# The second layer's MLP as seven products of quarters, with weight sums on GpSimd

## The chip, the cores and the metric

The kernel runs on one core of a Trainium2 chip. The metric is the device time of one launch in microseconds (us). Engines in the profile are PE (TensorE, matmuls), PEld (its weight loads), DVE (VectorE), ACT (ScalarE), POOL (GpSimd) and SP (SyncE, which issues most DMAs).

## What is computed

One inference step of a trunk of two layers over 640 tokens (512 sample tokens, then 128 prompt tokens), width D = 1024, MLP width 4096, all in float32. The first layer mixes by chunked gating and gated linear attention, the second by a recurrent block; each is followed by a squared-ReLU MLP, and every sub-layer has a norm ahead of it and one behind it:

```python
x = x + g1 * rmsnorm(y, norm_g[i, 1])
hff = rmsnorm(x, norm_g[i, 2]) * (1.0 + sc2) + sh2
f = jnp.square(jax.nn.relu(hff @ mlp_w1[i] + mlp_b1[i])) @ mlp_w2[i] + mlp_b2[i]
x = x + g2 * rmsnorm(f, norm_g[i, 3])
```

The shifts, scales and gates (sh, sc, g) differ between sample and prompt tokens. For the second layer (i = 1) the last line's x is the output.

## The kernel before

Every float32 operand of a large product is the sum of two float32r parts: `split` (L193) casts on ACT (L195) and subtracts on DVE (L196). A product is then three matmuls, `mm3` (L199): first weight part by both parts of the data, second weight part by the first part of the data (L201 to L203).

Weights come in slabs of 128 x 1024, 512 KB each. `prep` loads them in the order of use on SP's queue into raw buffers (three of them, `raw`), splits them and puts both parts into a slot of its class; `done` gives a slot back and calls `prep` again. So loads and splits run ahead as far as slots and raw buffers are free. A scheduler fixes one order of instructions for each engine when the program is built; each engine, and each DMA queue, then works in that order, and an instruction that waits holds what stands behind it.

`chain` (L336) finishes a token tile of 128 tokens: the norm behind a sub-layer (squares summed on ACT L342, products with the gate's rows on DVE L343), the residual x (L354), the next norm (ACT L357), eight transposes on PE (L333), scale and shift into hf (DVE L366, ACT L368), and the split of hf into `h1` and `h2`, feature-major. At the end of the kernel it writes the output instead (L351, L352). The token tiles come to the second MLP in the order 0, 1, 2, 4, 3.

The MLP, `mlp` (L1069), is called once for each layer. First product: a slab of W1 gives 128 of the 4096 hidden features for all tokens, in two halves of 320 tokens (`proj`), each eight feature tiles x 3 matmuls of 320 columns; ten slabs (six at the start, four at the end) go by token groups of 256 and 384 instead (`proj_groups`, `proj_group`), so that the first group can begin before all token tiles are there. ACT makes the square of the ReLU (L1068, L1069), then f is split. Second product: four slabs of W2 give all of y for one group of four hidden tiles; `ytile` makes, per token tile and half of 512 features, 4 x 3 matmuls of 512 columns, token-major, and DVE adds the bank to y in SBUF (L1103). `hgroup` and `ygroup` alternate, eight groups in all. In the last group the first three token tiles are finished (chain, output) ahead of the work on the others (L1129 to L1138).

`run` (L1166 on) ends with `out.send((wp, (1, 3), ExitStack()))`, which projects out of the recurrent block and runs the chains, and `self.mlp(1, mlp_i[1], xs, wp, None)` (L1221), which is the second layer's MLP. PSUM has six product banks and two others in this part. POOL issues the loads of slabs that the first layer had split ahead to memory (L165), the last of them at 862 us, and does nothing after that.

## Time and profile before

| | us |
|---|---|
| median of 3 runs | 1422.86 |
| lowest, highest | 1421.66, 1423.7 |
| span of the profiled execution | 1418.3 |

The span is from the first to the last instruction of one profiled execution. The runs' times lie 3.4 to 5.4 us above it. The mean granted TensorE clock of that execution was 0.998. The second MLP takes the time from about 960 us to the end.

| engine | busy us | share |
|---|---|---|
| PE | 1395.2 | 98% |
| DVE | 881.1 | 62% |
| ACT | 672.7 | 47% |
| POOL | 15.3 | 1% |

In the profile a group's row gives the busy time and the mean duration of one instruction, and then how long the engine was idle just before such instructions and what released it. In a timeline row the first number is the start and the second the duration; several instructions of one form are drawn together as x2, x4 and so on. Matmuls overlap: the time that one takes from the stream is the distance from its start to the next one's.

### The profile page before, as it was taken

The page shows a single profiled execution, that of the slowest core. Times are in us where ns is not written, and L with a number is a line of the kernel's source. Part 1 is how long each engine was busy: PE and PEld are TensorE (multiplying, and loading weights), DVE is VectorE, ACT ScalarE, POOL GpSimd, SP SyncE. Part 2 cuts the span into 40 slices and gives each one's busy share as a digit, 9 for nine tenths or more (in the row PEclk, how much of TensorE's full clock was granted, in tenths as well). Part 3 has the DMA queues.
Part 4 walks back from the last instruction along what each step waited for, and adds up shares of the span by engine and source line. Part 5 has one row for each costly group of instructions (what it writes and reads, how often), then busy time and mean ns, then how long its engine had stood idle before and what let it go on. Part 6 is the DMA issues. An engine that isn't in the chain of part 4 may idle for free.

```text
span 1418.3 us, 20181 instructions
## 1 busy us (share of the span) xinstructions
PE 1395.2 (98%) x8080; PEld 1243.8 (88%) x8080; DVE 881.1 (62%) x1407; ACT 672.7 (47%) x1217; POOL 15.3 (1%) x29
## 2 busy tenths in 40 slices
PE   7999999999999999999999999999999999999998
PEld 4788889889899898898889999879988989989896
DVE  5598858656768777787466798676342442433436
ACT  6744635675244154252267768867341522423142
POOL 2000000000000000000000000000000000000000
PEclk9999999999999999999999999999999999999999
DMA  9545317214577766766302442223231321212102
GB/s 370 177 153 179 130 64 265 92 45 144 168 250 243 264 224 229 272 202 213 138 31 104 153 151 99 89 76 107 102 105 45 104 73 61 99 35 104 60 30 75
DMA packets 60046, 195.89 MB, mean 138 GB/s; under 512 B 5888, under 2 KB 17632, under 8 KB 55344
## 3 DMA queue, kind: packets, MB, share of 16 engines
q1 hardware_dynamic: 57936, 179.92, 36.8%
q0 software_dynamic: 2016, 14.68, 3.0%
q8 instruction: 63, 1.03, 0.3%
q14 instruction: 31, 0.25, 0.1%
HBM read 176.97 MB, written 17.61 MB: 137 GB/s over the span
## 4 chain that ended last, share of the span: by engine, by line
PE 87%; DVE 5%; ACT 5%; issue 2%; DMA 2%; SPq 0%; DVEq 0%; ACTq 0%
PE mm L203 27%; PE mm L202 27%; PE mm L201 27%; PE aux L333 1%; DVE junk L244 1%; PE aux L823 1%; ACT h L195 1%; ACT w L195 1%; PE aux L808 1%; PE aux L442 1%; PE aux L818 1%; ACT r L135 1%; DVE w L196 0%; DMA x<-in_xs 0%; PE aux L681 0%
## 5 line engine op out<-in xcount | busy, mean ns | idle before, releaser
L201 PE MATMUL mm<-h,w 128*128 128x320 f32 (+2 forms) x1376 | 425.8, 310 | 3.4 <-ACT h L195 3.4
L202 PE MATMUL mm<-h,w 128*128 128x320 f32 (+2 forms) x1376 | 426.1, 310 | 0.6 <-DVE h L196 0.6
L203 PE MATMUL mm<-h,w 128*128 128x320 f32 (+2 forms) x1376 | 426.6, 310 | 0.0
L196 DVE TENSOR_TENSOR w<-raw,w 128x1024 fp32r<-128x1024 f32 x164 | 198.8, 1223 | 139.1 <-ACT w L195 138.0
L195 ACT CAST w<-raw 128x1024 fp32r<-128x1024 f32 x164 | 170.4, 1049 | 215.9 <-PE mm L203 120.7
L201 PEld LDWEIGHTS mm<-h,w 128*128 128x128 f32 x1376 | 258.6, 188 | 5.9 <-ACT h L195 3.7
L202 PEld LDWEIGHTS mm<-h,w 128*128 128x128 f32 x1376 | 259.2, 188 | 2.9 <-DVE h L196 1.2
L203 PEld LDWEIGHTS mm<-h,w 128*128 128x128 f32 x1376 | 259.2, 188 | 0.1
L244 DVE SCALAR_TENSOR_TENSOR junk<-raw,cond 128x1024 bf16<-128x1024 f32 x160 | 195.2, 1220 | 37.8 <-DMA raw<-in_modw 36.1
L202 PE MATMUL mm<-w,f 128*128 128x512 f32 x520 | 205.4, 395 | 0.0
L201 PE MATMUL mm<-w,f 128*128 128x512 f32 x520 | 205.1, 395 | 0.0
L203 PE MATMUL mm<-w,f 128*128 128x512 f32 x520 | 204.7, 395 | 0.0
L1103 DVE TENSOR_TENSOR y<-mm,y 128x512 f32<-128x512 f32 x140 | 95.7, 688 | 121.8 <-PE mm L203 121.8
L195 ACT CAST f<-r 128x320 fp32r<-128x320 f32 (+2 forms) x128 | 56.1, 459 | 235.5 <-PE mm L203 233.4
L203 PEld LDWEIGHTS mm<-w,f 128*128 128x128 f32 x520 | 97.6, 188 | 23.4 <-DVE f L196 0.2
L202 PEld LDWEIGHTS mm<-w,f 128*128 128x128 f32 x520 | 97.7, 188 | 22.6 <-DVE w L196 0.3
L201 PEld LDWEIGHTS mm<-w,f 128*128 128x128 f32 x520 | 97.7, 188 | 22.6
L1068 ACT ACTIVATE r<-mm,cols 128x320 f32<-128x320 f32 (+2 forms) x128 | 65.6, 524 | 66.6 <-PE mm L203 65.8
L196 DVE TENSOR_TENSOR f<-r,f 128x320 fp32r<-128x320 f32 (+2 forms) x128 | 60.2, 488 | 49.8 <-ACT f L195 48.7
L201 PE MATMUL mm<-w,h 128*128 128x512 f32 x220 | 86.9, 397 | 0.0
L202 PE MATMUL mm<-w,h 128*128 128x512 f32 x220 | 86.3, 393 | 0.0
L203 PE MATMUL mm<-w,h 128*128 128x512 f32 x220 | 85.6, 393 | 0.6 <-DVE h L196 0.6
(226 smaller groups left out, 1626.7 us busy)
## 6 DMA issues: line engine op xcount, KB each, us to landing
raw<-in_w SPq DMA_DIRECT2D x128, 512.0 KB, 3.4
raw<-in_modw SPq DMA_DIRECT2D x80, 512.0 KB, 4.3
ws<-w SPq DMA_DIRECT2D x14, 1024.0 KB, 5.2
w<-ws POOLq DMA_DIRECT2D x14, 1024.0 KB, 5.1
m<-in_mod SPq DMA_DIRECT2D x8, 1024.0 KB, 12.8
raw<-in_rgin SPq DMA_DIRECT2D x16, 512.0 KB, 4.9
raw<-in_evin_fm SPq DMA_DIRECT2D x12, 512.0 KB, 3.9
x<-in_xs SPq DMA_DIRECT2D x8, 512.0 KB, 5.0
```

The costliest lines, as they stand in the source:

```text
L135: self.tab = nc.scalar.activation(*args, **kw)
L195: i = self.nc.scalar.copy(d1, x)
L196: self.nc.vector.tensor_tensor(d2, x, d1.bitcast(F32), OP.subtract)
L201: nc.tensor.matmul(ps, w1, x1, start=start, stop=False)
L202: nc.tensor.matmul(ps, w1, x2, start=False, stop=False)
L203: nc.tensor.matmul(ps, w2, x1, start=False, stop=stop)
L244: nc.vector.scalar_tensor_tensor(self.junk, r, 1.0, self.cond[:, c, :], op0=OP.mult, op1=OP.mult, accum_out=self.modacc[:, l * 48 + j, c:c ...
L333: self.nc.tensor.transpose(ps[:, i * P:(i + 1) * P], xn[:, k * P:(k + 1) * P], self.ident)
L442: nc.tensor.matmul(ps[32 * j:32 * j + 32, :], cpad[:, kk, :], mods[k][:, kk, :], start=kk < 4, stop=kk >= 4, tile_position=(0, 32 * j))
L808: nc.tensor.matmul(ps[:, d * 256:(d + 1) * 256], ke[d][:, toks(t)], qe[d][:, :, toks(t)], start=True, stop=True)
L1068: nc.scalar.activation(r, ps, AF.Relu, bias=self.col(B1 + l * 32 + m))
L1103: nc.vector.tensor_tensor(ys[t][:, h, :], ps, b2row[:, h, :] if q == 0 else ys[t][:, h, :], OP.add)
```

## The change

The second layer's call of `mlp` is replaced by `smlp`, with its slabs planned by `smlp_plan`. Both matrix products are done by Strassen's scheme in Winograd's form: each of the three matrices is cut in four quarters, and seven products of sums of quarters replace the eight plain ones.

First product: the data's quarters are 4 feature tiles x 320 tokens of `hraw`, which the chains now leave feature-major and unsplit (`chain` writes it in place of hf, and each token tile's x to memory, `xd`). The sums of the data's quarters are four subtractions on DVE of 128 x 1280. The weights' sums are three POOL additions of 128 x 512 for each of 16 pairs of slabs (`sums`), one more for the slab called ya, which reads back a sum that POOL's queue has written to memory. For the first six pairs the products with the plain quarter (0, 0) come first (slabs e, `early`), since they need only the first 320 tokens. Each product is 192 matmuls of 320 columns. What the products add up to is added on DVE out of PSUM (or copied by ACT), and the four quarters of the hidden features stay in SBUF (`z`, 16 tiles of 128 x 2 x 640); ReLU and square on ACT.

Second product: W2's sums are again made on POOL (wb, wc one addition a slab, wa two and a write to memory), z's sums on DVE (t1 to t4) right ahead of their split (`fop`, 16 slots). y is feature-major, so weights stand still and 320 tokens stream. There are three phases of two products each, called b, a, c, in 16 steps of 24 matmuls, and a last product d in 16 steps of 12. At the end of a phase the banks go into y's quarters (`hraw` again): four copies on ACT (e1), 4 + 8 + 8 + 4 + 4 + 4 DVE operations of 128 x 320 (e7, e6, e5, e3, e2, e4). y is then transposed token tile by token tile (`finish`), and `chain` writes the output. Token tiles 3 and 4 are finished during d, tiles 0, 1 and 2 behind its last matmul. PSUM is changed to eight product banks ahead of the second product.

The second MLP has 112 slabs in place of 64, five slots, and a fourth raw buffer (every fourth is `rawx`). In the diff below, removed comments are left out.

```diff
     def raw(self):
+        self.nraw += 1
+        if self.rawx is not None and self.nraw % 4 == 0:
+            return self.rawx.tile([P, D], F32, name="raw", tag="raw", bufs=1)
         return self.rawp.tile([P, D], F32, name="raw", tag="raw", bufs=3)
...
+            if callable(src):
+                src(w)
+            elif i in self.ready:
...
         nc.vector.scalar_tensor_tensor(x, s2, rs, x, op0=OP.mult, op1=OP.add)
+        if self.hraw is not None:
+            nc.sync.dma_start(self.xd[t], x)
...
-        h = wp.tile([P, KD, P], F32, name="hf", tag="hf", bufs=2)
+        if self.hraw is None:
+            h = wp.tile([P, KD, P], F32, name="hf", tag="hf", bufs=2)
+        else:
+            h = self.hraw[:, :, toks(t)]
...
-        self.split(self.h1[:, :, toks(t)], self.h2[:, :, toks(t)], h)
+        if self.hraw is None:
+            self.split(self.h1[:, :, toks(t)], self.h2[:, :, toks(t)], h)
...
+        def sums(p):
+            t, u = self.raw(), self.raw()
+            load(t, lo, W1[2 * p][:, lo])
+            nc.sync.dma_start(u, W1[2 * p + 1])
+            nc.gpsimd.tensor_tensor(u[:, hi], u[:, lo], u[:, hi], OP.add)
+            nc.gpsimd.tensor_tensor(t[:, hi], u[:, hi], t[:, lo], OP.subtract)
+            nc.gpsimd.dma_start(s2d[p], t[:, hi])
+            nc.gpsimd.tensor_tensor(u[:, lo], t[:, lo], u[:, lo], OP.subtract)
+            return t, u
...
+        def wa(s, w):
+            u, t = self.raw(), self.raw()
+            nc.sync.dma_start(u, W2[2 * s])
+            load(t, lo, W2[2 * s + 1][:, hi])
+            nc.gpsimd.tensor_tensor(t[:, lo], u[:, hi], t[:, lo], OP.add)
+            nc.gpsimd.tensor_tensor(t[:, hi], t[:, lo], u[:, lo], OP.subtract)
+            nc.gpsimd.dma_start(s2d[self.NP + s], t[:, hi])
+            both(w, t)
...
+        op((0, 0), B(0, 0))
+        for p in range(NE):
+            ps = self.mm()[:, :HT]
+            prod(ps, ("e", p // 2), p % 2, (0, 0), True, True)
+            nc.scalar.copy(zq(p, 0, 0), ps)
+            if p % 2:
+                done(("e", p // 2))
+        tt(B(0, 1), B(1, 1), B(0, 1), OP.subtract)
+        tt(B(0, 0), B(0, 1), B(0, 0))
+        op((1, 0), B(0, 0))
+        op((0, 1), B(0, 1))
+        tt(B(0, 1), B(0, 0), B(1, 0), OP.subtract)
+        tt(B(0, 0), B(1, 1), B(0, 0), OP.subtract)
+        op((1, 1), B(0, 0))
...
+        for name, first, second in (("b", (0, lambda s: zq(s, 0, 0), e1), (1, t3, e7)),
+                                    ("a", (1, t2, e6), (0, t1, e5)),
+                                    ("c", (1, lambda s: zq(s, 1, 1), e3), (0, lambda s: zq(s, 1, 0), e2))):
+            ba, bb = [], []
+            for s in range(NP + 1):
+                if s < NP:
+                    step(s, (name, s), *first, ba)
+                if s:
+                    step(s - 1, (name, s - 1), *second, bb)
+                    done((name, s - 1))
...
+            if s == 12:
+                finish(3)
+            if s == 14:
+                finish(4)
+        for t in range(3):
+            finish(t)
...
         out.send((wp, (1, 3), ExitStack()))
-        self.mlp(1, mlp_i[1], xs, wp, None)
+        self.retire(self.rw)
         res.close()
-        pes.close()
+        xes.close()
+        self.smlp(1, mlp_i[1])
```

Where the second MLP begins, DVE before (x3 is token tile 3's residual, rs and hf belong to its norm and operand; h2 are second parts of the data's operand, f of the hidden features):

```order
L354 SCALAR_TENSOR_TENSOR x3_2046<-scr_8778,rs_8786,x3_2046 128x1024
L366 TENSOR_SCALAR hf_8682<-aux_8683,modv_122 128x128 x2
L366 TENSOR_SCALAR hf_8682<-aux_8692,modv_122 128x128 x2
L319 RECIPROCAL rs_8793<-sd_8792 128x1
L196 TENSOR_TENSOR h2_126<-hf_8682,h1_125 128x8x128
L366 TENSOR_SCALAR hf_8797<-aux_8798,modv_122 128x128 x2
L366 TENSOR_SCALAR hf_8797<-aux_8807,modv_122 128x128 x2
L196 TENSOR_TENSOR h2_126<-hf_8797,h1_125 128x8x128
L196 TENSOR_TENSOR f_8862<-r_8863,f_8862 128x256
L196 TENSOR_TENSOR f_8893<-r_8894,f_8893 128x256
```

DVE in the same place after, from the operand of tile 4 on (w are slabs, raw_8807 and raw_8818 hold sums of pairs 0 and 1, raw_8954 and raw_8993 of pairs 2 and 3, z0 is the first hidden tile pair):

```order
L381 TENSOR_SCALAR hraw_8480<-aux_8720,modv_154 128x128 x2
L381 TENSOR_SCALAR hraw_8480<-aux_8729,modv_154 128x128 x2
L329 RECIPROCAL rs_8844<-sd_8843 128x1
L205 TENSOR_TENSOR w_8919<-raw_8807,w_8919 128x512
L205 TENSOR_TENSOR w_8919<-raw_8818,w_8919 128x512
L381 TENSOR_SCALAR hraw_8480<-aux_8848,modv_154 128x128 x2
L381 TENSOR_SCALAR hraw_8480<-aux_8857,modv_154 128x128 x2
L1318 TENSOR_TENSOR hraw_8480<-hraw_8480 128x4x320 x2
L205 TENSOR_TENSOR w_8952<-raw_8954,w_8952 128x1024
L205 TENSOR_TENSOR h2_158<-hraw_8480,h1_157 128x4x320
L205 TENSOR_TENSOR w_8991<-raw_8993,w_8991 128x1024
L205 TENSOR_TENSOR h2_158<-hraw_8480,h1_157 128x4x320
```

The per-tile splits of hf are gone; the splits of whole quarters (128x4x320) stand between splits of slabs whose sums POOL makes.

The loads of pairs 2 and 3 on SP's queue after, between the writes of x to memory (none of these rows has a counterpart before):

```order
L366 DMA xd_8483<-x2_2073 128x1024
L1175 DMA raw_8818<-in_w1 128x512
L1185 DMA raw_8819<-in_w1 128x1024
L1175 DMA raw_8953<-in_w1 128x512
L366 DMA xd_8485<-x4_2083 128x1024
L1185 DMA raw_8993<-in_w1 128x1024
L366 DMA xd_8484<-x3_2078 128x1024
L1185 DMA raw_8954<-in_w1 128x1024
L1175 DMA raw_8992<-in_w1 128x512
```

The load into raw_8953 stands ahead of the other loads of these pairs, and a write of x waits between them.

POOL late in phase a after, where the first slab of c comes in between (L1240 to L1242 are a slab of a, L1249 one of c); before, POOL has no row in this part:

```order
L1240 TENSOR_TENSOR raw_11997<-raw_11996,raw_11997 128x512
L1241 TENSOR_TENSOR raw_11997<-raw_11997,raw_11996 128x512
L1242 DMA s2_101<-raw_11997 128x512
L1249 TENSOR_TENSOR raw_12076<-raw_12076 128x512
L1240 TENSOR_TENSOR raw_12037<-raw_12036,raw_12037 128x512
L1241 TENSOR_TENSOR raw_12037<-raw_12037,raw_12036 128x512
```

For each slab of a, two additions and one DMA were added, for each of c one addition.

The end of PE's order before (mm_12223 is the last bank of token tile 4):

```order
L201 MATMUL mm_12223<-xp_6824,f_11879 128x512
L202 MATMUL mm_12223<-wlo_8201,f_11879 128x512
L203 MATMUL mm_12223<-xp_6824,f_11879 128x512
L201 MATMUL mm_12223<-w_11946,f_11910 128x512
L202 MATMUL mm_12223<-w_11946,f_11910 128x512
L203 MATMUL mm_12223<-w_11946,f_11910 128x512
```

and after (mm_12805 is the last bank of product d, L1482 are transposes of y):

```order
L210 MATMUL mm_12805<-h1_157,w_12908 128x320
L211 MATMUL mm_12805<-h2_158,w_12908 128x320
L212 MATMUL mm_12805<-h1_157,w_12908 128x320
L1482 MATMUL mm_13123<-ident_141,hraw_8480 128x128 x4
L1482 MATMUL mm_13128<-ident_141,hraw_8480 128x128
L1482 MATMUL mm_13147<-ident_141,hraw_8480 128x128 x4
L1482 MATMUL mm_13128<-ident_141,hraw_8480 128x128
L1482 MATMUL mm_13152<-ident_141,hraw_8480 128x128 x2
L1482 MATMUL mm_13171<-ident_141,hraw_8480 128x128 x2
L1482 MATMUL mm_13128<-ident_141,hraw_8480 128x128
```

Before, nothing follows the last matmul with weights; after, the transposes of token tiles 0, 1 and 2 do.

## Rows read from the trace of the kernel before

**Rows 1.** The page: PE's busy time, and the chain's shares by line.

```profile
PE 1395.2 (98%) x8080; PEld 1243.8 (88%) x8080; DVE 881.1 (62%) x1407; ACT 672.7 (47%) x1217; POOL 15.3 (1%) x29
PE mm L203 27%; PE mm L202 27%; PE mm L201 27%; PE aux L333 1%; DVE junk L244 1%; PE aux L823 1%; ACT h L195 1%; ACT w L195 1%; PE aux L808 1%; PE aux L442 1%; PE aux L818 1%; ACT r L135 1%; DVE w L196 0%; DMA x<-in_xs 0%; PE aux L681 0%
```

**Rows 2.** Windows; columns: stretch, length, busy PE, PEld, DVE, ACT, POOL, clock, DMA share, GB/s.

```profile
1100.00:1150.00 50.00, 50.00 (x288) 45.83 (x287) 18.73 (x24) 18.35 (x32) 0.00 (x0) 1.00 0.26 85
...
1411.00:1418.30 7.30, 0.36 (x2) 0.00 (x0) 3.12 (x6) 1.02 (x3) 0.00 (x0) 0.84 0.20 76
```

**Rows 3.** Timeline of PE: three starts, 192 and then 120 matmuls apart.

```profile
1047.40 0.31 PE L201 MATMUL mm<-h,xp 128*128 128x320 f32 x1
...
1075.56 0.39 PE L201 MATMUL mm<-w,f 128*128 128x512 f32 x1
...
1103.45 0.31 PE L201 MATMUL mm<-h,xp 128*128 128x320 f32 x1
```

**Rows 4.** Timeline where the second MLP begins: last token tiles' operands.

```profile
961.08 1.50 ACT L368 ACTIVATE hf<-aux,modv 128x128 f32<-128x128 f32 x4
...
972.91 0.16 DVE L319 RECIPROCAL rs<-sd 128x1 f32<-128x1 f32 x1 [1.57 <-ACT sd L135]
...
974.92 1.09 PE L333 MATMUL aux<-ident,scr 128*128 128x128 f32 x8
...
976.44 1.50 ACT L368 ACTIVATE hf<-aux,modv 128x128 f32<-128x128 f32 x4 [0.85 <-DVE hf L366]
...
979.24 0.62 PE L201 MATMUL mm<-h,w 128*128 128x384 f32 x2 [0.75 <-ACT h L195]
980.50 0.44 PE L202 MATMUL mm<-h,w 128*128 128x384 f32 x1 [0.64 <-DVE h L196]
```

**Rows 5.** Groups by line and form, 980 to 1418 us: slab and operand splits.

```profile
L196 DVE TENSOR_TENSOR w<-raw,w 128x1024 fp32r<-128x1024 f32 x41 | 49.8, 1224 | 87.8 <-ACT w L195 87.7
...
L195 ACT CAST w<-raw 128x1024 fp32r<-128x1024 f32 x41 | 42.5, 1047 | 66.8 <-PE mm L203 66.2 <-DMA raw<-in_w 0.5
...
L196 DVE TENSOR_TENSOR f<-r,f 128x320 fp32r<-128x320 f32 x44 | 20.5, 489 | 12.0 <-ACT f L195 11.5
...
L195 ACT CAST f<-r 128x320 fp32r<-128x320 f32 x44 | 19.0, 458 | 149.0 <-PE mm L203 148.5
```

**Rows 6.** DMA issues: count, KB each, median us from issue to landing.

```profile
raw<-in_w SPq DMA_DIRECT2D x128, 512.0 KB, 3.4
```

**Rows 7.** Timeline of POOL, then of DVE, near the kernel's start.

```profile
10.08 1.42 POOL L566 MEMSET attm<- 128x512 f32 x2 [9.63 <-DMA x<-in_xs]
...
18.45 0.63 POOL L575 MEMSET kdt<- 64x640 f32 x1 [0.33 <-PE aux L333]
...
21.27 1.11 POOL L571 MEMSET qe<- 64x640 f32 x1 [1.08 <-PE aux L333]
22.42 0.63 POOL L572 MEMSET qe<- 64x640 f32 x1
...
18.37 1.26 DVE L477 TENSOR_SCALAR x<-x,rs 128x1024 f32<-128x1024 f32 x1
...
21.06 0.75 DVE L477 TENSOR_SCALAR x<-x,rs 128x1024 f32<-128x1024 f32 x1
...
22.10 1.23 DVE L196 TENSOR_TENSOR w<-raw,w 128x1024 fp32r<-128x1024 f32 x1
```

**Rows 8.** Timeline of the kernel's end: last matmul, last token tile on DVE.

```profile
1410.96 0.40 PE L203 MATMUL mm<-w,f 128*128 128x512 f32 x1
...
1412.12 0.69 DVE L343 TENSOR_TENSOR y<-y,grow 128x512 f32<-128x512 f32 x1
...
1413.65 1.42 DVE L351 SCALAR_TENSOR_TENSOR x<-y,rs,x 128x512 f32<-128x512 f32 x2
```

More of the change, by code (lines that the diff above doesn't have):

```diff
@@ L309, in gate_rows @@
         grow = wp.tile([P, 2, D], F32, name="grow", tag="grow", bufs=1)
+        grow = [grow[:, c, :] for c in range(2)]
         self.get_rows((l, part), grow)
@@ L504, in start @@
                 self.put_rows("c", ccol)
-                self.get_rows("c", self.cond)
+                self.get_rows("c", [self.cond[:, c, :] for c in range(2)])
             part_b(k)
@@ L1139, in mlp, with smlp_plan, load, add @@
         es.close()
+    NP = 16
+    NE = 6
+    def smlp_plan(self, l):
+        nc, W1, W2 = self.nc, self.A["w1"][l], self.A["w2"][l]
+        pl, idx = self.plan, {}
+        lo, hi = slice(0, 512), slice(512, D)
+        s2d = [self.dram.tile([P, 512], F32, name="s2") for _ in range(2 * self.NP)]
+        held = {}
+        def load(t, c, src):
+            nc.sync.dma_start(t[:, c], src)
+        def add(key, f):
+            idx[key] = len(pl)
+            pl.append((f, "b"))
+        def sums(p):
[7 more added lines that the diff above has]
+            return t, u
+        def both(w, t):
+            self.split(w[:, 0, :], w[:, 1, :], t)
+        def early(j, w):
+            t = self.raw()
+            for i in range(2):
+                load(t, (lo, hi)[i], W1[2 * (2 * j + i)][:, lo])
+            both(w, t)
+        def late_a(p, w):
+            held[p] = sums(p)
+            both(w, held[p][1])
+        def late_b(j, w):
+            for i, c in enumerate((lo, hi)):
+                self.split(w[:, 0, c], w[:, 1, c], held.pop(2 * j + i)[0][:, hi])
+        def xa(p, w):
+            held[p] = sums(p)
+            both(w, held[p][0])
+        def xb(p, w):
+            both(w, held.pop(p)[1])
+        def ya(p, w):
+            t = self.raw()
+            load(t, lo, W1[2 * p][:, hi])
+            load(t, hi, s2d[p])
+            nc.gpsimd.tensor_tensor(t[:, hi], t[:, lo], t[:, hi], OP.subtract)
+            both(w, t)
+        def yc(j, w):
+            t = self.raw()
+            for i in range(2):
+                load(t, (lo, hi)[i], W1[2 * (2 * j + i) + 1][:, hi])
+            both(w, t)
+        def wb(s, w):
+            t = self.raw()
+            nc.sync.dma_start(t, W2[2 * s])
+            nc.gpsimd.tensor_tensor(t[:, hi], t[:, lo], t[:, hi], OP.subtract)
+            both(w, t)
+        def wa(s, w):
[5 more added lines that the diff above has]
+            nc.gpsimd.dma_start(s2d[self.NP + s], t[:, hi])
+            both(w, t)
+        def wc(s, w):
+            t = self.raw()
+            load(t, lo, W2[2 * s + 1][:, lo])
+            load(t, hi, s2d[self.NP + s])
+            nc.gpsimd.tensor_tensor(t[:, hi], t[:, lo], t[:, hi], OP.subtract)
+            both(w, t)
+        def wd(j, w):
+            t = self.raw()
+            for i in range(2):
+                load(t, (lo, hi)[i], W2[2 * (2 * j + i) + 1][:, hi])
+            both(w, t)
+        def bind(f, i):
+            return lambda w: f(i, w)
+        for j in range(self.NE // 2):
+            add(("e", j), bind(early, j))
+        for j in range(self.NE // 2):
+            for p in (2 * j, 2 * j + 1):
+                add(("xb", p), bind(late_a, p))
+                if p % 2:
+                    add(("s2", j), bind(late_b, j))
+        for p in range(self.NE, self.NP):
+            add(("xa", p), bind(xa, p))
+            add(("xb", p), bind(xb, p))
+        for p in range(self.NP):
+            add(("ya", p), bind(ya, p))
+            if p % 2 == 0:
+                add(("yc", p // 2), bind(yc, p // 2))
+        for key, f, n in (("b", wb, 16), ("a", wa, 16), ("c", wc, 16), ("d", wd, 8)):
+            for s in range(n):
+                add((key, s), bind(f, s))
+        return idx
@@ L1219, in run @@
         next(odd, None)
+        res2 = ExitStack()
+        hr = self.pool("hr", res2, side="right")
+        self.hraw = hr.tile([P, KD, T], F32, name="hraw")
+        self.xd = [self.dram.tile([P, D], F32, name="xd") for _ in range(NT)]
+        self.rawx = hr
+        self.b2c = hr.tile([P, 16], F32, name="b2c")
+        nc.sync.dma_start(self.b2c, A["b2c"])
         out.send((wp, (1, 3), ExitStack()))
-        self.mlp(1, mlp_i[1], xs, wp, None)
+        self.retire(self.rw)
         res.close()
-        pes.close()
+        xes.close()
+        self.smlp(1, mlp_i[1])
+        res2.close()
+        self.pes.close()
 def _cols(a):
```

177 lines of the change are left out of this document (171 added, 6 removed).

## The prediction

> **What bounds the kernel now.** First the busy shares and the chain of waits: TensorE (PE) is busy in 98% of the span, and three matmul lines make up 81% of the chain [rows 1]. Then the table of stretches: in the middle of the second MLP, PE is busy for all of 50 us, VectorE (DVE) for 18.73 and ScalarE (ACT) for 18.35, GpSimd (POOL) not at all, at 85 GB/s [rows 2]. So there a matmul less is time less, and the other engines have room. A matmul's busy time is not its cost, since they overlap; its cost is the distance of two starts. 192 matmuls of 320 columns start between 1047.40 and 1075.56, 0.1467 us each; 120 of 512 columns between 1075.56 and 1103.45, 0.2324 [rows 3]. That is 0.458 and 0.454 ns a column: cost goes by columns, and weight loads are hidden.
>
> **What the matmuls give.** Before, the second MLP has 1056 matmuls of 320 columns (22 slabs x 2 halves x 24), 240 of 256 and 240 of 384 (10 slabs by token groups; on average 320) and 960 of 512: 154.9 + 70.4 + 223.1 = 448.4 us. After, seven products of 192 in each layer of it are 2688 of 320 columns: 394.3. PE's gain is 54 us, and the span was 1418.3; 40 transposes come back, of which 24 lie behind the last matmul and 16 cost some 2 us (8 take about 1.09 [rows 4]). What is left to find out is how much of the 54 the edges and the other engines take.
>
> **The start.** Before, PE never needs all tokens at once: it begins with the first 256, and loses 0.75 and 0.64 us to the last ones [rows 4]. After, the first products (72 matmuls, 10.6 us) need the first 320 tokens, hence token tile 2, whose modulated operand is written from 961.08 [rows 4]; with a cast and a subtract of 128x1280 (1.25 times a 128x1024 cast, and 1.224 [rows 5] x 1.25) they begin at about 965.5 and end at about 976. Everything else needs sums of quarters over all tokens, and the last operand tile is written from 976.44 [rows 4]: about 978. From there the order decides. On DVE the quarters' splits alternate with two weight splits of POOL's sums. Those sums' loads stand on SP's queue behind the load into raw_8953; by the rotation of raw buffers this needs a buffer that is only given back by a split standing, on DVE, behind the square root's reciprocal of token tile 3, at 972.91 now [rows 4]: about 974. With 3.4 us from issue to landing [rows 6], the pair of loads is there at about 978, four POOL sums of about 1.1 end near 983, cast and subtract near 985.7, the first quarter's subtract near 987, the second weight split and third quarter near 990, the last quarter, two subtractions and a split later, near 995. One group of 12 matmuls runs in between. So I take the other 2604 matmuls to start at about 996 and to last 381.9: 1378. Against the clean start (965.5 + 394.3 = 1360) this is 18 us lost. If the loads came earlier, the quarters alone (978 plus five operations of about 1.5 each on DVE) would still hold PE to about 986: 8 to 18 is the range here.
>
> **The middle.** One step of the second stage has 24 matmuls, 3.52 us. DVE, by rows: a weight split 1.224, two operand splits of 0.489, and in the first phase two sums of the same size [rows 5]: 3.18. In the phase called a 2.20, in c 2.69. DVE is under PE in all, ACT too (1.047 + 2 x 0.458 [rows 5]). Four slabs and eight operand slots stand ahead, so a burst of evacuations (e6 and e5: 16 of 128x320 and two slab splits, some 10 us) is mostly covered; I put 2 us for it, 2.5 for the first slab of sums that is not prefetched (pair 4 of the first stage) and 1.5 for the rest. The gaps will also let the granted clock fall: it is 0.84 in the stretch after the last matmul, where PE idles [rows 2]; I put 1.5 us for the restart after the long wait. With the 2 us of transposes: 1378 + 9.5 = 1387.5.
>
> **POOL's sums** have no row: before, POOL only writes constants and issues DMAs. Their price is bounded by a two-input 128x512 operation on DVE, 0.69 [rows 8], from below, and by two passes of writing 128x512 on POOL, 1.42, from above [rows 7]; I take 1.1, nearer the upper one, since POOL is the slower engine in rows 7. A step has one sum in the first phase and in c, two in a: 2.2 of 3.52 us. By the upper end it is 2.84, still under it. In the first stage three sums per pair, 3.3 of 7.04 us. [...]
>
> **The end.** Before, after the last matmul (its start 1410.96, so 1411.4) one token tile's chain is left, 6.9 us to 1418.3 [rows 8]. After, three token tiles are left. Four evacuations (about 0.5 each, 2), the first transposes (1.1), then on DVE per tile two products of 0.69, two of 1.41 together [rows 8] and two small ones, about 3.1: 9.3, and 3.2 from the start of the last write's halves to the end as before. That is about 16, 9 more than now. At least the DVE work and the last write remain, 13; at most the three chains stand one behind the other, 20.
>
> **The sum.** 1387.5 + 16 = 1403.5 for the span. The runs of before lie 3.4 to 5.4 us above the profiled span (median 1422.86 against 1418.3): add 4.5, so 1408. The bounds of the start (8 to 18, minus up to 10), of the end (-3 to +4) and twice the 7.5 us of stalls give 1395 to 1420.
>
> **Rivals.** *A: POOL and DVE shut each other out.* In the trace a DVE operation that takes 0.75 alone takes 1.26 beside a POOL write that begins with it, and another time the POOL write takes 1.11 instead of 0.63; a two-input DVE subtract of 1.23 next to POOL writes loses nothing on either side [rows 7]. So some pairs exclude each other and some do not; sums that read two buffers on POOL beside DVE operations that read two buffers have no row. The mechanism: DVE's splits and operand sums all read two SBUF buffers, so if they exclude POOL's sums, a step costs their sum once the lead is used up: 3.18 + 1.1 = 4.3 in the first phase, 2.2 + 2.2 = 4.4 in a, 2.69 + 1.1 = 3.8 in c, against 3.52. Over 16 steps each that is 68 + 70 + 61 = 199 against 169 us, 30 more; the lead of four slabs takes back up to 14, the first stage adds 4 or 5. So 1428 to 1443 with the rest of the forecast as it is; taking 1430. It ends on the slow side; with a price of 0.75 a sum (63 + 59 + 56 = 178, 9 more than PE) it would be hidden by the lead and come out at the forecast, which is the point from which it decides. For it: the two stretched rows. Against it: the undisturbed one. [...]
>
> *B: the raw buffers bound phase a.* A slab there needs two raw buffers of four: a load (3.4 [rows 6]), two sums (2.2), a write back of a half and the split (2.3), 8 to 9 us for two slabs in flight, against 7.04: 8 us more over the phase, 1416. For it: SP issues in order, so one late buffer holds all. Against it: the write back is only 256 KB.
>
> *C: the start is hidden better* than I read from the order, and the waits of the middle do not appear: 965.5 + 394.3 + 8 (quarters) + 4 + 16 + 4.5 = 1393.
>
> That the change does not do what it says (fewer matmuls) is excluded by the order: PE has 2688 there.
>
> **How the numbers follow.** Forecast 0.42, A 0.40, B 0.11, C 0.07. A is nearly as likely because every DVE operation of the second stage has the form in question. A measurement of this kernel can tell some 0.2% (2.85 us) from no change. Faster: forecast 0.38, A 0.05, B 0.07, C 0.07 = 0.57. Same: 0.03 + 0.06 + 0.03 = 0.12. Slower: 0.01 + 0.29 + 0.01 = 0.31. The likeliest case's own range is 1395 to 1420; the range that leaves out no more than 2 in 10 reaches from there to 1440, most of A's.
>
> **What would show it.** Of the start: a PE gap of some 20 us behind the 72 first matmuls, ended by a DVE split that itself waited for ACT's cast of a POOL sum; a gap of 8 or less is C. Of the middle: 50 us of PE busy per 50 us in the first phase and in a, as now [rows 2]; under A the splits and POOL's sums both show means well above 1.22 and 1.1, and PE waits for DVE all through. Under B, DVE and ACT wait for DMA or POOL while SP waits for buffers. Of the end: 16 us between the last matmul with weights and the last write. The forecast is wrong if a POOL sum takes over 1.7 us (two are then over 3.4 of the 3.52 us a step in phase a), with or without exclusion.

## The result, and the profile after

The changed kernel takes 1461.06 us (median; 1456.42 to 1461.57) against 1422.26 us before: 1.0267 times the time, 95% interval 1.0251 to 1.0284. The prediction said 1408 with a range to 1440. The profiled execution took 1456.42 us, the shortest of the four, and the other three 1460.76 to 1461.57; its span is 1454.7.

The page of the kernel after (the lines that answer to [rows 1]; the second is the chain's shares by engine):

```profile
PE 1365.4 (94%) x8312; PEld 1250.3 (86%) x8312; DVE 1045.1 (72%) x1620; ACT 756.9 (52%) x1358; POOL 260.7 (18%) x189
PE 69%; DVE 10%; POOL 6%; ACT 6%; DMA 5%; issue 3%; SPq 0%; DVEq 0%; POOLq 0%; ACTq 0%
```

PE has 30 us less of busy time than before, and is idle for 89 us of the span instead of 23. That is not the 54 us of the matmul count: 40 transposes come in, and behind its waits PE often runs at a lower granted clock (0.72 over the start and 0.88 over phase a, in the stretches below). The chain, 87% PE before, now has POOL, DMA and DVE in it. Where that happens is read from the stretches (columns as in [rows 2]). In order: the start; phases b, a and c of the second product; what follows the last matmul with weights.

```profile
967.00:998.00 31.00, 17.89 (x99) 16.83 (x100) 24.01 (x27) 17.11 (x34) 11.60 (x9) 0.72 0.30 104
1191.00:1252.00 61.00, 57.42 (x383) 55.91 (x382) 50.98 (x85) 29.27 (x54) 38.13 (x14) 1.00 0.36 119
1252.00:1349.00 97.00, 66.97 (x385) 63.66 (x384) 53.73 (x63) 32.93 (x59) 58.74 (x49) 0.88 0.56 179
1349.00:1408.00 59.00, 57.64 (x386) 56.39 (x385) 53.33 (x81) 30.86 (x50) 27.29 (x12) 1.00 0.59 199
1438.30:1454.70 16.40, 2.97 (x24) 2.29 (x22) 11.59 (x26) 4.86 (x16) 0.00 (x0) 0.74 0.35 129
```

The three phases have 384 matmuls each, 56.3 us of work at 0.1467. Phase a takes 97. From here on the loss of a stretch is its length less 0.1467 us for each of its 320-column matmuls, from the first product of the new MLP (967.59) on. The stretches end at the 192nd, 768th, 1344th, 1728th (end of b), 2112th (a), 2496th (c) and 2688th (d):

| | start | to 768 | to 1344 | b | a | c | d |
|---|---|---|---|---|---|---|---|
| loss, us | 19.6 | 6.5 | 0.0 | 5.1 | 40.9 | 2.6 | 1.8 |

967.6 + 394.3 + 76.4 = 1438.3, and 16.4 behind it. Phase a holds over half of the loss. Of its 40.9 us PE waits 29.9, and for the rest it is busy longer than its work (66.97 us in the window for 56.3). PE's longest waits there (queue, line, releaser, us in total, times, longest):

```profile
PE mm L210 <- ACT w L204: 12.1, 5, 3.7
PE mm L212 <- DVE w L205: 9.0, 6, 1.6
PE mm L210 <- ACT hraw L1425: 8.2, 1, 8.2
```

The first two are waits for slabs. The third is at the head of the phase: PE needs a bank that ACT copies into y, and ACT's four copies stand behind the cast of a slab that has not had its sums yet. Behind this wait two matmuls start 0.267 us apart and not 0.1467 (the granted clock is 0.50 from 1255.0 to 1265.3, and 1.00 from 1266 to 1292):

```profile
1258.95 1.04 ACT L204 CAST w<-raw 128x1024 fp32r<-128x1024 f32 x1 [2.60 <-POOL raw L1241]
1259.90 1.40 ACT L1425 COPY hraw<-mm 128x320 f32<-128x320 f32 x4
1260.37 0.64 PE L210 MATMUL mm<-h,w 128*128 128x320 f32 x1 [8.21 <-ACT hraw L1425]
...
1261.07 0.47 PE L212 MATMUL mm<-h,w 128*128 128x320 f32 x1
1261.34 0.47 PE L210 MATMUL mm<-h,w 128*128 128x320 f32 x1
```

This is a pair of its slabs on POOL (two sums, L1240 and L1241, and the issue of the write of a half sum, L1242), up to the next pair's first sum:

```profile
1286.98 1.26 POOL L1240 TENSOR_TENSOR raw<-raw 128x512 f32<-128x512 f32 x1 [4.21 <-DMA raw<-in_w]
1288.32 1.26 POOL L1241 TENSOR_TENSOR raw<-raw 128x512 f32<-128x512 f32 x1
1289.88 0.56 POOL L1242 DMA_DIRECT2D s<-raw  x1 [0.30 <-POOL raw L1241]
1290.46 1.28 POOL L1240 TENSOR_TENSOR raw<-raw 128x512 f32<-128x512 f32 x1
1291.82 2.15 POOL L1241 TENSOR_TENSOR raw<-raw 128x512 f32<-128x512 f32 x1
1294.27 0.56 POOL L1242 DMA_DIRECT2D s<-raw  x1 [0.30 <-POOL raw L1241]
1298.80 1.29 POOL L1240 TENSOR_TENSOR raw<-raw 128x512 f32<-128x512 f32 x1 [3.97 <-DMA raw<-in_w]
```

and SP's queue beside it (x2: two issues drawn together, the second at about 1294; L1238 loads a slab into the first raw buffer u, L1175 a half into the second, t):

```profile
1289.61 4.71 SPq L1238 DMA_DIRECT2D raw<-in_w  x2
1294.43 5.20 SPq L1175 DMA_DIRECT2D raw<-in_w  x2
```

Sum after sum, then 3.97 us in which POOL waits for a load, and round again: 1298.80 - 1286.98 = 11.8 us for two slabs, for which PE needs 7.04. From 1262 to 1326 such pairs begin 11.8 to 12.7 us apart, with the granted clock at 1.00 in between (12.1 us each, from 1274.84 and from 1298.80) or at 0.86 (11.8 from 1286.98, 11.9 from 1310.89), so it is the ring that sets the pace there. The load for which POOL waits was issued at 1294.43. Two things end there: the write issued at 1289.88 lands and gives the first slab's t back, and SP comes past the load into the next u, which the second slab's second sum held until 1293.97. SP's own waits in phase a say the same:

```profile
SPq L1175 <- DMA s<-raw: 41.8, 10, 4.5
SPq L1238 <- POOL raw L1241: 32.9, 12, 4.6
```

The other new thing is in the durations. Groups by form from 960 us on (busy us, mean ns, idle before; the slab split and the operand split were 1224 and 489 ns in [rows 5]):

```profile
L205 DVE TENSOR_TENSOR w<-raw,w 128x1024 fp32r<-128x1024 f32 x106 | 156.6, 1480 | 92.2 <-ACT w L204 92.1
L205 DVE TENSOR_TENSOR h<-z,h 128x320 fp32r<-128x320 f32 x112 | 69.3, 659 | 0.6 <-ACT h L204 0.6
L1318 DVE TENSOR_TENSOR z<-z,mm 128x320 f32<-128x320 f32 x48 | 22.5, 478 | 2.0 <-PE mm L1307 1.9
...
L1233 POOL TENSOR_TENSOR raw<-raw 128x512 f32<-128x512 f32 x16 | 42.2, 2648 | 27.4 <-DMA raw<-in_w 22.2 <-DVE z L1318 2.1 <-DVE h L205 2.0
L1241 POOL TENSOR_TENSOR raw<-raw 128x512 f32<-128x512 f32 x16 | 25.9, 1616 | 1.3
```

Both splits and POOL's sums are stretched; DVE's sums with one input in PSUM (mm) are not, at 478 ns (479 in e5 below, without sums on POOL). Sorted by what DVE did beside them, 37 POOL sums without a two-input SBUF operation of DVE beside them took 1.25 to 1.30 us, some of these beside DVE operations that read PSUM; 39 with 1.2 to 3 us of such operations beside them took 1.94 on average. Slab splits of DVE without a sum beside them took 1.22 us (41 of them), with over 1 us of sums beside them 1.77 (34). (Operations that the timeline draws singly, 950 to 1410 us.)

### The profile page after: what moved, and what is told of

It reads as the page before. It is cut to its first block, busy times and chain, and to the rows that moved or that the text cites. A ratio compares the mean times of both kernels' runs of the same rounds, so it can differ in the third digit from the quotient of the medians.

```text
span 1454.7 us, 21633 instructions
## 1 busy us (share of the span) xinstructions
PE 1365.4 (94%) x8312; PEld 1250.3 (86%) x8312; DVE 1045.1 (72%) x1620; ACT 756.9 (52%) x1358; POOL 260.7 (18%) x189
## 4 chain that ended last, share of the span: by engine, by line
PE 69%; DVE 10%; POOL 6%; ACT 6%; DMA 5%; issue 3%; SPq 0%; DVEq 0%; POOLq 0%; ACTq 0%
PE mm L212 18%; PE mm L211 18%; PE mm L210 18%; DMA raw<-in_w 3%; PE mm L1306 3%; PE mm L1305 3%; PE mm L1307 3%; DVE w L205 2%; POOL raw L1241 2%; ACT w L204 2%; POOL raw L1240 1%; POOL raw L1233 1%; DVE junk L253 1%; DVE z L1318 1%; PE aux L343 1%
## 5 line engine op out<-in xcount | busy, mean ns | idle before, releaser
L210 PE MATMUL mm<-h,w 128*128 128x320 f32 (+2 forms) x1408 | 441.1, 314 | 27.4 <-ACT w L204 12.5
L212 PE MATMUL mm<-h,w 128*128 128x320 f32 (+2 forms) x1408 | 441.0, 313 | 10.2 <-DVE w L205 10.1
L211 PE MATMUL mm<-h,w 128*128 128x320 f32 (+2 forms) x1408 | 439.0, 312 | 0.0
L205 DVE TENSOR_TENSOR w<-raw,w 128x1024 fp32r<-128x1024 f32 (+1 forms) x233 | 306.9, 1326 | 145.4 <-ACT w L204 144.3
L204 ACT CAST w<-raw 128x1024 fp32r<-128x1024 f32 (+1 forms) x233 | 239.8, 1036 | 297.6 <-PE mm L212 85.8
L210 PEld LDWEIGHTS mm<-h,w 128*128 128x128 f32 x1408 | 267.9, 191 | 33.1 <-ACT w L204 14.1
L212 PEld LDWEIGHTS mm<-h,w 128*128 128x128 f32 x1408 | 268.0, 190 | 12.8 <-DVE w L205 12.6
L211 PEld LDWEIGHTS mm<-h,w 128*128 128x128 f32 x1408 | 268.2, 190 | 1.5 <-issue 0.9
L1305 PE MATMUL mm<-h,w 128*128 128x320 f32 x448 | 141.2, 317 | 22.4 <-ACT h L204 18.3
L1306 PE MATMUL mm<-h,w 128*128 128x320 f32 x448 | 141.0, 315 | 2.3 <-DVE h L205 2.2
L1307 PE MATMUL mm<-h,w 128*128 128x320 f32 x448 | 140.5, 314 | 0.0
L174 POOL DMA_DIRECT2D w<-ws x14 | 7.6, 540 | 739.8 <-DVE y L353 638.8
L211 PE MATMUL mm<-w,f 128*128 128x512 f32 x320 | 126.4, 395 | 0.0
L210 PE MATMUL mm<-w,f 128*128 128x512 f32 x320 | 126.1, 395 | 0.0
L212 PE MATMUL mm<-w,f 128*128 128x512 f32 x320 | 125.8, 395 | 0.0
L1305 PEld LDWEIGHTS mm<-h,w 128*128 128x128 f32 x448 | 86.4, 194 | 23.9 <-ACT h L204 19.0
L1306 PEld LDWEIGHTS mm<-h,w 128*128 128x128 f32 x448 | 86.2, 192 | 3.0 <-DVE h L205 3.0
L1307 PEld LDWEIGHTS mm<-h,w 128*128 128x128 f32 x448 | 86.1, 192 | 0.0
## 6 DMA issues: line engine op xcount, KB each, us to landing
m<-in_mod SPq DMA_DIRECT2D x8, 1024.0 KB, 11.9
```

What stands on the lines that cost most here:

```text
L204: i = self.nc.scalar.copy(d1, x)
L205: self.nc.vector.tensor_tensor(d2, x, d1.bitcast(F32), OP.subtract)
L210: nc.tensor.matmul(ps, w1, x1, start=start, stop=False)
L211: nc.tensor.matmul(ps, w1, x2, start=False, stop=False)
L212: nc.tensor.matmul(ps, w2, x1, start=False, stop=stop)
L1305: nc.tensor.matmul(ps, w[:, 0, c], x1, start=start and kk == 0, stop=False, skip_group_check=True)
```

## The experiments

Two theories on the 40.9 us of phase a, and on the rest. **Ring (R)**: a slab holds two of four raw buffers through a load, two sums, a write and a split; the loop through the buffers is longer than PE's work on two slabs. **Exclusion (X)**: POOL's sums and DVE's operations with two SBUF inputs keep each other out, so that the two engines' times add up. The table has the losses as above, the time and the ratio, with its interval, to runs of the kernel before made beside it; "first" is the start of the first product. The losses are those of one profiled execution each, while the runs of one kernel spread over 2.8 to 8.6 us, so a difference of two or three us in one column is not to be read. "First" holds up to 3 us of what happened ahead of the MLP: the residual x of the first token tile (L364) stands at 933.2 to 936.3. Counted from there the first product comes after 33.3 to 33.7 us with the first layer's sums on POOL, after 26.5 with them on DVE, and after 28.8 to 29.7 with more pairs first.

| kernel | first | start | to 768 | b | a | c | us | ratio |
|---|---|---|---|---|---|---|---|---|
| after | 967.6 | 19.6 | 6.5 | 5.1 | 40.9 | 2.6 | 1461.1 | 1.027 (1.025 to 1.028) |
| e1, a's sums on DVE | 968.2 | 21.4 | 6.0 | 5.7 | 32.3 | 0.0 | 1446.9 | 1.017 (1.015 to 1.019) |
| e2, six raw buffers in a | 966.9 | 21.9 | 6.3 | 7.5 | 20.7 | 7.5 | 1446.4 | 1.017 (1.015 to 1.019) |
| e3, no slab subtract in a | 966.7 | 19.7 | 6.7 | 6.6 | 36.0 | 4.6 | 1454.8 | 1.023 (1.022 to 1.025) |
| e11, e2 and e3 | 967.2 | 19.5 | 6.7 | 8.3 | 10.3 | 8.3 | 1435.0 | 1.010 (1.008 to 1.012) |
| e4, all sums on DVE | 962.2 | 21.1 | 2.8 | 4.0 | 17.8 | 4.3 | 1426.3 | 1.003 (1.002 to 1.004) |
| e5, e2 and e4 | 959.8 | 21.4 | 3.0 | 5.8 | 2.2 | 8.3 | 1416.1 | 0.997 (0.995 to 0.998) |
| e7, e4, a's write by ACT | 961.5 | 19.0 | 2.7 | 3.7 | 13.6 | 0.1 | 1419.2 | 0.998 (0.997 to 1.000) |
| e8, e5, first layer on POOL | 970.0 | 21.3 | 6.5 | 1.2 | 3.6 | 7.4 | 1421.0 | 1.000 (0.999 to 1.001) |
| e6, e5, ten pairs first | 965.1 | 15.6 | 1.0 | 7.5 | 0.0 | 7.3 | 1406.0 | 0.990 (0.988 to 0.991) |
| e9, e6, writes by ACT | 964.2 | 14.9 | 2.4 | 4.4 | 0.0 | 7.0 | 1409.0 | 0.991 (0.989 to 0.993) |
| e10, e9, fourteen pairs | 962.7 | 7.9 | 4.6 | 8.3 | 0.0 | 6.1 | 1404.4 | 0.988 (0.986 to 0.990) |

Part of a's loss is PE's waits, and part the lower clock behind them:

| phase a | after | e1 | e2 | e3 | e11 | e4 | e7 | e5 |
|---|---|---|---|---|---|---|---|---|
| PE waits, us | 29.9 | 21.5 | 12.8 | 23.0 | 5.3 | 12.7 | 9.2 | 1.0 |
| granted clock | 0.88 | 0.90 | 0.91 | 0.85 | 0.95 | 1.00 | 0.98 | 1.00 |

**e1: phase a's two sums on DVE.**

```diff
         def wa(s, w):
...
-            nc.gpsimd.tensor_tensor(t[:, lo], u[:, hi], t[:, lo], OP.add)
-            nc.gpsimd.tensor_tensor(t[:, hi], t[:, lo], u[:, lo], OP.subtract)
+            nc.vector.tensor_tensor(t[:, lo], u[:, hi], t[:, lo], OP.add)
+            nc.vector.tensor_tensor(t[:, hi], t[:, lo], u[:, lo], OP.subtract)
```

> The two weight sums of each slab of phase a go to DVE; all else as in the changed kernel (1461 us). Theory R (ring): phase a loses 40 us because a slab holds two of four raw buffers through load, sums, write to memory and split, so that two slabs take 11.9 us in place of 7.04; the write of a half by POOL's queue stays (about 4.5 us to landing), so a pair still takes some 10 to 11 us and the time falls by only 7 to 15 us, to 1446 to 1454. Theory X (exclusion): POOL's sums and DVE's operations with two SBUF inputs shut each other out; with the sums on DVE a step costs DVE 2.2 + 1.38 = 3.6 us against 3.52 of PE, and the 40 us fall to under 8: 1425 to 1432.

1446.9 us, a's loss 32.3: as R had it. DVE's sums take 0.69 us, and eight pairs still take 88.6 us. DVE waits for loads, and SP for the write's landing (SP's waits from 1262 to 1340, then one of DVE's):

```profile
SPq L1175 <- DMA s<-raw: 42.8, 12, 6.7
```

```profile
1296.40 0.69 DVE L1240 TENSOR_TENSOR raw<-raw 128x512 f32<-128x512 f32 x1 [2.96 <-DMA raw<-in_w]
```

**e2: two more raw buffers in phase a**, in the quarters of y that are not written before its end; POOL as in the changed kernel.

```diff
-            u, t = self.raw(), self.raw()
-            nc.sync.dma_start(u, W2[2 * s])
+            t = self.raw()
+            u = self.hraw[:, 4 * (s % 2):4 * (s % 2) + 4, HT:HT + 256]
+            t4 = t.rearrange("p (a b) -> p a b", a=4)
+            nc.sync.dma_start(u, W2[2 * s].rearrange("p (a b) -> p a b", a=4))
```

> Phase a's first buffer u comes from two free quarters of y, so that six raw buffers are in use there; sums stay on POOL. R: four slabs are in flight, the loop no longer binds; what is left is the shared time of DVE and POOL, about 4.8 us a step (77 against 56 us), so about half of the 40 us comes back: 1438 to 1446. X alone: buffers do not matter, 1455 to 1461.

1446.4 us, just above R's range; a's loss halved to 20.7, while c, behind it, lost 5 us more: part of the gain was given back there. X alone fails here, since the buffers matter. The phase takes 77.0 us, the 77 that the two engines' times add up to; but that is no proof of the sum, since SP still waits for POOL's second sum to give u back, which has two buffers of its own only:

```profile
SPq L1240 <- POOL raw L1243: 43.9, 11, 7.9
```

**e3: phase a without DVE's slab subtracts.**

```diff
-            both(w, t)
+            nc.scalar.copy(w[:, 0, :], t)
+            nc.scalar.copy(w[:, 1, :], t)
```

> Leaves out the residual part of phase a's weights: ACT writes both parts as casts, so DVE has no slab subtract there (0.98 us of two-input operations a step are left); the sums stay on POOL, the buffers as they were. R: the loop stays, only the stretch of the second sum (0.9 us a pair) goes: 1450 to 1456. X: POOL's 2.6 us and DVE's 0.98 fit in 3.52, and 30 us or more come back: 1421 to 1432.

1454.8 us, a's loss 36.0, as R had it. POOL's sums in the phase are back at 1.28 us on average (1.50 in the changed kernel), so nothing stretches them any more, and a pair of slabs still takes 10.7 to 12.1 us. 1.22 us less of DVE work a step (and a cast of 1.05 more on ACT) gives 5 us in all, 6.9 of PE's waits: with four buffers not the sum of the two engines' times binds, but the loop.

**e11: e2 and e3 together** (the same part left out as in e3): what is left with the loop loosened.

> Six raw buffers in phase a with the sums on POOL, and again the residual parts of phase a's weights left out (ACT casts both parts). With six buffers phase a still loses 20.7 us. If that rest is exclusion (2.2 us of DVE's two-input operations and 2.6 of sums a step do not fit in 3.52), it falls to under 8 us, since 0.98 and 2.6 do: 1430 to 1436. If the rest is POOL itself, its DMA issues or the loads, it stays: 1443 to 1448.

1435.0 us. Phase a's loss falls from 20.7 to 10.3, where the same edit gave 4.9 with four buffers. So exclusion is the second limit. That it counts for more once the ring is loosened holds for the loss, but not for PE's waits, which fall by 7.5 us here and by 6.9 with four buffers; the rest is the clock, 0.95 here and 0.85 in e3. 10.3 is above the 8 that I gave. Little of what is left can be exclusion, since the sums take 1.33 us on average (1.62 in e2). SP still waits for u, which points to its two buffers and the sums' own time; that was not tried by itself:

```profile
SPq L1240 <- POOL raw L1243: 35.6, 11, 5.7
```

**e4: all 128 sums on DVE.**

```diff
-            nc.gpsimd.tensor_tensor(u[:, hi], u[:, lo], u[:, hi], OP.add)
+            nc.vector.tensor_tensor(u[:, hi], u[:, lo], u[:, hi], OP.add)
```

and so for the other seven lines of this kind.

> All 128 weight sums on DVE, none on POOL. X: no sum and no split is stretched any more; the long sums in phase b (10 us) go, the start gains 5 to 7 us since four sums of 0.69 replace four of 1.3 to 2.5; DVE then has 127 us of work in phases b and a against 113 of PE, partly covered by the lead: 1412 to 1428. R: as e1, and some 10 us more from the start and phase b: 1435 to 1445.

1426.3 us: in X's range, and 9 us below R's. It is better than e1 in four places: the first product starts 6.0 us earlier (7.1, counted from the residual), the stretch to 768 loses 3.2 less, b 1.7 less, and a 14.5 less. The rows of both divide these 14.5. The first sum of a's slabs stands 13.9 us ahead of the phase in e4 (1229.46 and 1243.35) and 9.2 in e1 (1245.93 and 1255.18); the likeliest reason is that b's sums no longer hold the slabs up, which was not tried. From the first to the last slab's first sum it is 78.6 us in place of 81.4. Behind that the phase takes 9.4 us in place of 16.4, since c's first sums, still on POOL in e1, fall in there: ACT casts c's first slab ahead of a's last one and waits for POOL's sum, and the two splits take 4.46 us, 2.35 in e4 (from e1):

```profile
1329.16 1.40 POOL L1249 TENSOR_TENSOR raw<-raw 128x512 f32<-128x512 f32 x1 [5.12 <-DMA raw<-in_w]
1330.60 1.99 ACT L204 CAST w<-raw 128x1024 fp32r<-128x1024 f32 x2 [5.40 <-POOL raw L1249]
1331.67 4.46 DVE L205 TENSOR_TENSOR w<-raw,w 128x1024 fp32r<-128x1024 f32 x2 [0.76 <-ACT w L204]
```

So e1 had not taken exclusion out of the end of phase a, and R's range for e4, which was built on e1, was too high by that among other things. In a, t is again loaded only when the write of its half lands (SP's waits from 1243 to 1317; then an issue of the write on POOL and the next load into t, 4.1 us apart):

```profile
SPq L1175 <- DMA s<-raw: 48.9, 15, 5.1
```

```profile
1280.73 0.54 POOL L1242 DMA_DIRECT2D s<-raw  x1 [5.66 <-DVE raw L1241]
...
1284.81 0.33 SPq L1175 DMA_DIRECT2D raw<-in_w  x1
```

**e5: e2 and e4 together.**

> All sums on DVE and six raw buffers in phase a: both causes taken away together. Phase a loses 40.9 us in the changed kernel, 20.7 with the buffers alone, 17.8 with all sums on DVE alone. If ring and exclusion are two causes of which either alone keeps half, phase a is then bound by DVE, 3.6 us a step against 3.52, and loses under 4 us: 1426 less 14 to 17, that is 1409 to 1413, faster than before (1422). If DVE is the bound already when the sums are there (it has 127 us of work in phases b and a against 113), little comes back: 1420 to 1426.

1416.1 us, 3 above the expected range and faster than before. With both taken away phase a loses 2.2 us, where e2 left 20.7 and e4 17.8. Moving the sums does two things, which no run separates in all: it ends the exclusion (slab splits take 1.22 us on average, 1.48 in the changed kernel), and a sum takes 0.69 us in place of 1.28; e11 (10.3) lies about half way. What the expectation missed is c, which now loses 8.3: DVE is busy for 57.42 of 65 us there, and PE waits once, 4.5 us, for the burst of evacuations between a and c, with a granted clock of 0.95 (the window, and a row of the waits in it):

```profile
1302.00:1367.00 65.00, 59.84 (x389) 59.42 (x389) 57.42 (x99) 30.55 (x51) 0.00 (x0) 0.95 0.60 197
```

```profile
PE mm L210 <- DVE hraw L1320: 5.2, 2, 4.5
```

**e8: as e5, but with the first layer's sums on POOL again.** Lines L1186 to L1221 as in the changed kernel.

> Sums on POOL in the first stage, on DVE in the second, six raw buffers in phase a. Exclusion in the first stage costs what the kernels with all sums on DVE gain there: some 4 us at the start and 4 us up to the sixteenth pair: 6 to 10 us slower than with all on DVE and six buffers, 1416 to 1422. If POOL's sums cost nothing there, the same time.

1421.0 us, in the range: 4.9 us slower than e5 on the same chip, where I had put 6 to 10 (the profiled executions are 9.9 us apart, and that of e8 is the slowest of its ten). The first product starts 10.2 us later, 7.2 counted from the residual, and the stretch to 768 loses 3.5 more; phases b and c give some of it back. The start shows how: besides the sums' own time, DVE's residual x (L364) of token tile 4, which reads two SBUF buffers, took 1.28 before and takes 2.09 beside a sum in the changed kernel, as in e8:

```profile
962.08 2.09 DVE L364 SCALAR_TENSOR_TENSOR x<-scr,rs,x 128x1024 f32<-128x1024 f32 x1
```

**e7: as e4, with phase a's write of a half sum on ACT's queue.**

> All sums on DVE, four raw buffers, but the write of a half sum in phase a is issued on ACT's queue in place of POOL's. With all sums on DVE a raw buffer is loaded again 4.1 us after POOL issues that write. If the write's landing is what closes the loop (ring), a faster write shortens phase a by up to 2 us a pair, 8 to 16 in all: 1411 to 1419. If the loop is closed by the split on DVE, nothing changes: 1424 to 1428.

1419.2 us, at the upper edge of what R gave, but not by the way it gave: the write is no faster on ACT's queue (4.3 us to landing in phase a, 4.0 on POOL's). SP waits less for it all the same, and why was not settled:

```profile
SPq L1175 <- DMA s<-raw: 26.4, 14, 4.0
```

22 us less of that wait gave 4.2 us of a's loss, since SP then waits longer for u and for splits (24 us in place of 11). Another 4.2 us was saved in c, which I had not expected: PE waits 2.0 us in e4 for the evacuations behind a, with a granted clock of 0.97 over c, and not at all in e7. Why they come in time there stays open. The profiled execution of e7 is the fastest of its ten, 4.6 us under the median, so both savings may be less.

**e6: as e5, with ten instead of six pairs first** (`NE = 10`).

> As the kernel with all sums on DVE and six raw buffers, and ten instead of six pairs in the first products (120 matmuls, 17.6 us), which need only the first 320 tokens. Theory of the start: PE waits 5 to 10 us behind the first 72 products for the quarters, whose splits stand behind slab splits, so 7 us more of work there fill that wait: 5 to 7 us faster than with six pairs. Rival: the wait is for buffers and slots that the first products hold (five slots), and it moves behind them unchanged: no gain.

1406.0 us, 10 us faster than e5 on the same chip, more than expected. But the profiled executions are only 4.2 us apart (that of e6 is the slowest of its four), and in them the 192nd product ends at the same time (1009.4 in e5, 1008.8 in e6: 5.8 less is lost, from a first product 5.3 later). What they show is 2.0 less to 768 and 2.2 less in a. So the gain is there, and this profile does not show that it is the covered wait.

**e9: as e6, with all writes on ACT's queue**, and **e10: the same with fourteen pairs first**.

> All sums on DVE, six raw buffers in phase a, ten pairs first, and all writes of half sums issued on ACT's queue. With six buffers phase a loses nothing any more (0.0 us with ten pairs), so the faster write has nothing left to shorten there: within 2 us of the kernel with ten pairs (1406), unless the writes in the first stage hold buffers too, which would show up as up to 5 us there: 1401 to 1407.

> The same with fourteen pairs first (168 matmuls, 24.6 us). With ten pairs PE still loses 11.4 us between the 72nd and the 192nd product, at the quarters' splits. If PE's wait is for DVE's fixed queue of work (sums, splits, quarters) in front of the last quarter, 7 us more of first products cover up to 7 us of it: 1398 to 1402. If the slabs of the first products take that DVE time themselves (two more of 1.2 us, and slots), about 2 to 4 us: 1402 to 1405.

1409.0 and 1404.4 us. The writes bring nothing with six buffers, as expected: e9's time is 2 above the range that I gave, and its ratio lies in e6's interval. Fourteen pairs do cover the wait: the start loses 7.9 instead of 14.9, and the 192nd product ends at 998.8 instead of 1007.3. Of these 8.5 us, b and the stretch to 768 take back 6, so that the time lies in the second of the two ranges, that of the slabs which take DVE's time themselves; whether it is they that cost it was not read. e10 is the fastest kernel of the study: 0.988 of before (0.986 to 0.990). Its phase a has PE busy throughout, with POOL doing nothing (window as in [rows 2]):

```profile
1237.00:1293.00 56.00, 56.00 (x384) 55.92 (x382) 49.96 (x83) 29.03 (x49) 0.00 (x0) 1.00 0.71 232
```

## Why the prediction was wrong

*PE's gain* was right: 576 matmuls of the first layer ran in 84.5 us and 192 of d in 28.2 plus 1.8 for transposes, at 0.1467 each. *The end* was right: 16 us predicted, 16.4 measured. *The start* was right in its chain of causes and, in part by luck, in size: 18 us of loss predicted, 19.6 measured, beginning at 967.6 where 965.5 was predicted. The sign that I gave, a gap of some 20 us, did not show. The first 72 products end at 982.3 and not at 976, since they begin at a lower clock (0.86 granted from 967.6 to 982.3) and token tiles' transposes stand between them; PE then waits 10.3 and 2.2 us. So 13 us of the loss are waits. Most of the rest lies in the lower clock (0.81 granted from 967.6 to 1015.2) and in transposes, for which the prediction put 1.5 and 2 us elsewhere. The rows show its mechanism with one other name: the load that came late was that into raw_8954, not raw_8953. SP issued it at 977.60, when the DVE split of 976.88 behind token tile 3's reciprocal (976.37) had given a buffer back. POOL's first sum of pair 2 waits for it; ACT casts that pair's sum at 987.26, PE gets the second quarter at 992.53 and its second part at 995.33 (predicted: about 987 and 996):

```profile
981.00 1.29 POOL L1186 TENSOR_TENSOR raw<-raw 128x512 f32<-128x512 f32 x1 [8.56 <-DMA raw<-in_w]
...
987.26 1.04 ACT L204 CAST w<-raw 128x1024 fp32r<-128x1024 f32 x1 [4.53 <-POOL raw L1189]
988.33 3.00 DVE L205 TENSOR_TENSOR w<-raw,w 128x1024 fp32r<-128x1024 f32 x1 [2.23 <-ACT w L204]
...
992.53 0.63 PE L1305 MATMUL mm<-h,w 128*128 128x320 f32 x1 [10.27 <-ACT h L204]
995.33 0.64 PE L1306 MATMUL mm<-h,w 128*128 128x320 f32 x1 [2.16 <-DVE h L205]
```

*The middle* is the step that failed. It compared each engine's work in a step with PE's 3.52 us, found DVE (3.18, 2.20, 2.69) and POOL (2.2) under it, and put 7.5 us for stalls and the clock over all of it. Measured are 55 us from the 192nd to the last matmul of c. Two of its terms can be named: the 2 us for bursts of evacuations, of which one wait in front of phase a alone took 8.2, and the 1.5 us for the clock, where PE is busy for 67 us in phase a with 56.3 of work. How much of that time it would have waited at full clock is open. In phase a POOL, under the bound on average (two sums of 1.50 us in a step of 3.52), still bound, since its work lies in a loop with waits. The loop of a buffer t is load 4.4, two sums 2.6, wait ahead of the write 0.3, issue and landing of the write and the next load's issue 4.5: 11.8 us, with two slabs in it.

*Rival B* had this loop, and its sign (SP waits for buffers) showed, but it was mis-sized. It gave 8 to 9 us for two slabs "in flight", hence 8 us of loss and 0.11 of the chances. The term that was mis-sized is the write back: 2.3 us for it and the split together, and as an argument against B that it is only 256 KB. Its size did not tell its time: it takes 4.4 us to landing (median of 15 in phase a) and is what SP waits for most. The load took 4.4 and not 3.4, the two sums 2.6 and not 2.2.

*Rival A* was right in its mechanism and in that it decides for "slower" (1.017 in e2, with exclusion and more buffers; 1.003 in e4, without POOL's sums and with the ring), and wrong in where it counts. It charged 12, 14 and 5 us to b, a and c. In b and c the loss is 5.1 and 2.6 us in all; in a, DVE's slab subtracts beside the sums cost 4.9 while the ring binds (e3), and 10.4 with two more buffers (e2 against e11), about 7 us of PE's waits in both. At the start and in the first layer I had put 4 or 5; e8 against e5 gives 4.9. No row of before shows that such sums and splits exclude each other. This trace does: sums on POOL and DVE operations with two SBUF inputs stretch each other (1.28 to 1.94, 1.22 to 1.77 us), and those with an input in PSUM stay at 478 ns. What I charged for it, the sum of the two engines' times in each step, was not what bound the changed kernel; with six buffers it fits phase a (77.0 us in e2 for 77) but not once the subtracts are gone (66.6 in e11, where 2.6 + 0.98 a step would give 57).

*POOL's price*, 1.1 in the prediction, is 1.28 undisturbed, within its bounds (0.69 [rows 8] and 1.42 [rows 7]), between which I had taken 1.1. With the stretch a sum takes 1.50 us on average in phase a, under the 1.7 that were to be the sign of a wrong forecast: the forecast failed without that sign.

*The range* ended at 1440 because forecast, A and B were alternatives, each with the others' terms at zero. They happened together: the ring of B, with sums stretched by A, behind the start of the forecast. (*C* did not happen; its sum is 1392 and not 1393.)

## What to carry to other kernels

For a stage that is fed through a small ring of buffers, add up the loop of one buffer (load, every operation, a write back to its landing, and what the issuing queue holds in front of the next load) and compare that with the consumer's time; engine totals under the bound (here two sums of 1.50 us on POOL in a step of 3.52) said nothing about it. Look too at what stands in the same queue behind the instruction that waits: here ACT's copies of four banks did, and PE waited 8.2 us for them. Moving elementwise work to GpSimd beside VectorE operations that read two SBUF buffers cost more here than doing it on VectorE, at 0.69 instead of 1.28 us or more a sum (1426.3 us in e4 for 1461.1), even though VectorE was the busier engine. Fewer matmuls paid here only once start, ring and sums were mended: 54 us less of PE gave 39 us of loss first and 17 us of gain (1421.75 to 1404.43) at the end.
